# Attention units with four block pairs of keys: the fourth pair is transposed right behind the third

## The chip, the core and the metric

One core of a Trainium2 chip runs the whole kernel in one launch. The metric is device time in microseconds (us), and less is better. Engines in the text: TensorE (PE in the profile; its weight loads are PEld), VectorE (DVE), ScalarE (ACT), GpSimd (POOL) and SyncE (SP, which issues most DMAs). TensorE writes its results to PSUM, of which this kernel uses eight banks of 128 x 512 fp32; ScalarE and VectorE read them from there.

## The reference

One layer of a hybrid decoder, 1024 tokens by 1024 channels. One projection gives pool inputs, queries, keys, values and forget gates; half of the width goes through trailing means, the other half through causal attention with 8 heads of 64 channels and a bias from the gates. Then come an output projection with layer norm and an MLP with squared ReLU and a second layer norm.

```python
h = x @ w_in                                   # pool | q | k | v | forget gate
s = einsum('bhqd,bhkd->bhqk', q, k) * scale    # per head, causal
s = s + cq[..., :, None] - cf[..., None, :]    # cf = cumsum(log sigmoid(f))
p = softmax(where(kpos <= qpos, s, NEG_INF))
attn = einsum('bhqk,bhkd->bhqd', p, v)
x = layer_norm(ALPHA * x + concat([pool_out, attn]) @ w_out)
x = layer_norm(ALPHA * x + square(relu(x @ w_mlp1)) @ w_mlp2)
```

## The kernel before

All matrix products work on fp32 values that are split into a high and a low part (`split`: ScalarE copies the high part, VectorE subtracts to get the low part), and most take three matmuls (`three`).

Attention works by units `(p, e, m)`: head pair `p` (4), head `e` of it (2), and group `m` (4) of 256 queries. That is 32 units; for the first three head pairs a head's units run with m = 3, 2, 1, 0, for the last pair m rises. A unit with group m needs the keys of `m + 1` block pairs (a pair is 256 keys), so only a unit with m = 3 has four pairs; there are eight such units. For a unit, `att_probs` makes the scores on TensorE (L351, L352), adds the gate bias and takes the row minimum on VectorE (L357), and exponentiates on ScalarE (L359). One unit later `att_values` turns the probabilities and multiplies them with the values, all into one PSUM bank `ov` of the tag `pv`, of which there is one.

`turned(jp)` in `att_values` does one block pair: it takes a PSUM bank of tag `pt` (two buffers) and an SBUF tile `tt` of tag `A` (nine buffers), issues the transposes (L379: four, or three for a unit's last pair, the one on the diagonal), lets ScalarE copy the high part out (L380) and VectorE subtract the low part (L381). For the last pair GpSimd also clears a corner of `tt` (L377). The value passes of a pair are four matmuls of 256 columns (L395): two with the high part, which wait for L380, and two with the low part, which wait for L381. Once all passes are done, ScalarE and VectorE read `ov` (L400, L401) and SP stores the result (L402). Below, a unit's pairs are called first to fourth; "fourth turn" is the three transposes of the fourth pair, "third passes" are the four value passes of the third.

Between the passes, `fillstep` issues a piece of other TensorE work: the query and key projection of the next head pair (L83 to L85, bank tag `mm`), or in the last head pair the last pool group. After the units of the last head pair, the output projection follows.

The order on each engine is not that of the code: a scheduler fixes it before the run, engine by engine, from the code's order as a priority and from its own durations; it also puts in the semaphore waits and picks the buffers. Each engine then runs its list strictly in that order. In the code before, the second turn is issued ahead of the first passes, the third ahead of the second passes, and the fourth ahead of the third passes: one turn ahead at all times.

Of the kernel before, what the change touches and what calls it, by code (L numbers as in the profile page):

```python
# [36 lines left out]
def trunk(ctx, tc, xT, xn, wuqk, wvf, bf, poolw, pscale, wout, g1, b1, w1, w2, g2, b2, out):  # L37
# [13 lines left out]
    def slot(tag, shape, dt=F32R):  # L51
        uid[0] += 1
        return sb.tile([P] + list(shape), dt, tag=tag, bufs=NBUF[tag], name=f"{tag}{uid[0]}")
# [9 lines left out]
    def bank(tag=None):  # L63
        uid[0] += 1
        if tag is None:
            tag = CYCLE[rr[0] % 8]
            rr[0] += 1
        return ps.tile([P, CH], F32, tag=tag, bufs=PBUF[tag], name=f"{tag}{uid[0]}")
# [293 lines left out]
    def att_values(p, e, m, prob):  # L362
        h = 2 * p + e
        rows = slice(e * HD, (e + 1) * HD)
        orow = slice((1 - e) * HD, (2 - e) * HD)
        ov = bank("pv")[:, 0:256]

        def turned(jp):
            tp = bank("pt")
            tt = slot("A", [2, CH])  # L370
            if jp < m:
                blocks = [(jj * 256 + ii * P, 2 * jp + jj, ii) for jj in range(2) for ii in range(2)]
                ev = slice(0, CH)
            else:
                blocks = [(P, 2 * jp + 1, 1), (2 * P, 2 * jp, 0), (3 * P, 2 * jp, 1)]
                ev = slice(P, CH)
                nc.gpsimd.memset(tt[:, :, 0:P].bitcast(F32), 0.0)  # L377
            for col, j, ii in blocks:
                nc.tensor.transpose(tp[:, col : col + P], prob[ii][:, j * P : (j + 1) * P], ident)  # L379
            nc.scalar.copy(tt[:, 0, ev], tp[:, ev])  # L380
            nc.vector.tensor_tensor(tt[:, 1, ev], tp[:, ev], tt[:, 0, ev].bitcast(F32), ALU.subtract)  # L381
            return tt

        nxt = turned(0)
        for jp in range(m + 1):
            tt = nxt
            if jp < m:
                nxt = turned(jp + 1)
            fillstep()
            mov = ((0, 256), (256, CH)) if jp < m else ((256, CH), (0, 256))  # L390
            for s in range(2):
                for jj in range(2):
                    j = 2 * jp + jj
                    a, b = mov[jj]
                    nc.tensor.matmul(  # L395
                        ov, V[j][:, h].rearrange("p s d -> p (s d)"), tt[:, s, a:b],
                        start=(j == 0 and s == 0), stop=(j == 2 * m + 1 and s == 1),
                    )
        mx = slot("U", [256], F32)
        nc.scalar.copy(mx[rows], ov[orow])  # L400
        nc.vector.tensor_tensor(mx[rows], ov[rows], mx[rows], ALU.add)  # L401
        nc.sync.dma_start(mix_dram[m, rows, NG + p, :], mx[rows])  # L402
        if p == NPAIR - 1:
            row_scales(h, 2 * m, 2)
        elif m == 0:
            row_scales(h, 0, NT)

    def row_scales(h, i, n):
        ri = small([P, NT], "ri", bufs=2)
        nc.vector.reciprocal(ri[:, :n], rsum[h][:, i : i + n])  # L410
        tp = bank("pt")
        nc.tensor.transpose(tp[0:n, 0:P], ri[:, :n], ident)
        row = small([NT, P], "row")
        nc.scalar.copy(row[0:n], tp[0:n, 0:P])
        nc.sync.dma_start(rin_dram[h, i * P : (i + n) * P].rearrange("(i q) -> i q", q=P), row[0:n])
# [14 lines left out]
    def fillstep():  # L430
        fill["credit"] += fill["rate"]
        while fill["credit"] >= 1.0:
            fill["credit"] -= 1.0
            next(fill["gen"], None)
# [4 lines left out]
    for n, unit in enumerate(order):  # L439
        p = n // 8  # L440
        if n % 8 == 0:
            if p + 1 < NPAIR:
                gen, pieces, over = qk_proj(p + 1, "mm"), 4 * KT + 1, 28
            else:
                gen, pieces, over = last_fill(), (2 * KT + 2) * len(LATE), 14
            fill.update(gen=gen, credit=0.0, rate=pieces / over)
        prob = att_probs(*unit)
        if n + 1 < len(order):
            gate_row(2 * order[n + 1][0] + order[n + 1][1])
        if pend is None:  # L450
            for g in EARLY[1:]:
                pool_linear(g, "A")
        fillstep()
        if pend is not None:
            att_values(*pend)
        pend = (*unit, prob)
        if n % 8 == 7:
            run(gen)
    att_values(*pend)


# [390 lines left out]
    tt = nc.vector.tensor_tensor  # L852
# [303 lines left out]
```

## Time and profile before

| what | us |
|---|---|
| median of three runs (1041.37 to 1043.55) | 1042.59 |
| the profiled execution's own time | 1041.99 |
| its span, from the first instruction to the last | 1040.2 |
| TensorE busy in the span | 1018.5 |
| VectorE busy | 760.9 |
| ScalarE busy | 510.6 |

The attention units lie from about 117 to 326 us. The units with m = 3 have their passes at 120 (unit 1 below), 145 (2), 173 (3), 198 (4), 227 (5), 250 (6), 312 (7) and 319 us (8); 7 and 8 are those of the last head pair. In rows of the timeline, instructions of one line that follow each other on an engine are merged into one row: the first number is the start of the first, the second the time to the end of the last, `x4` their count, and brackets hold idle time of the engine before the row and what ended it. A matmul's shown duration is longer than its share of TensorE, since matmuls overlap; what one costs is read from the distance of the starts. On TensorE that is how a stall shows that leaves no idle time in the brackets.

### The profile page before, as it was taken

To read this page: it belongs to the slowest core of one execution; us is meant where nothing else is said; L and a number is where in the kernel's file an instruction comes from. 1 tells how busy PE (TensorE), PEld (TensorE's weight loads), DVE (VectorE), ACT (ScalarE), POOL (GpSimd) and SP (SyncE) were. 2 spreads that over 40 slices of the span, in tenths; PEclk is the share of its full clock that TensorE was granted. 3 is DMA by queue.
4 is the path that set the end of the run, shared out by engine and by line. 5 is a ranking of instruction groups with operands and counts; after the bars stand their busy time and mean duration, and the time that the engine had idled before them with its cause. 6 is when DMAs were issued, how large, how long until landed. Compare 5 with 4: busy or idle time off the path is not lost.

```text
span 1040.2 us, 14026 instructions
## 1 busy us (share of the span) xinstructions
PE 1018.5 (98%) x4976; PEld 846.2 (81%) x4976; DVE 760.9 (73%) x1303; ACT 510.6 (49%) x820; POOL 136.9 (13%) x236
## 2 busy tenths in 40 slices
PE   9999999999989999999999999999999999999996
PEld 9988888878768888887888888888788888888885
DVE  4576677777886897988888778788875566566547
ACT  4423666666774321676666766768631221122152
POOL 0000112111000021112122122120100000000047
PEclk9999999999999999999999999999999999999998
DMA  6302211111346542139757667565999888878753
GB/s 224 105 27 99 87 51 52 34 50 54 115 150 189 183 162 94 60 128 349 280 226 276 226 251 275 217 266 188 340 318 308 279 262 285 274 222 275 237 190 122
DMA packets 111798, 195.81 MB, mean 188 GB/s; under 512 B 9256, under 2 KB 77672, under 8 KB 111728
## 3 DMA queue, kind: packets, MB, share of 16 engines
q1 hardware_dynamic: 95456, 136.58, 40.2%
q0 software_dynamic: 15840, 57.68, 14.3%
q8 instruction: 39, 0.64, 0.3%
q10 hardware_dynamic: 432, 0.66, 0.2%
q14 instruction: 31, 0.25, 0.1%
HBM read 127.18 MB, written 67.70 MB: 187 GB/s over the span
## 4 chain that ended last, share of the span: by engine, by line
PE 52%; DVE 5%; DMA 2%; issue 1%; ACT 0%; DVEq 0%; SPq 0%
PE s L957 15%; PE s L603 9%; PE pv L957 8%; PE pt L603 6%; PE mm L603 6%; PE pv L603 4%; PE pt L957 2%; PE mm L957 2%; DMA S<-in_w_dram 1%; DVE B L72 1%; DMA A<-hid_dram 1%; DVE Q L72 0%; DVE A L726 0%; DVE bns L506 0%; DVE A L712 0%
## 5 line engine op out<-in xcount | busy, mean ns | idle before, releaser
L71 ACT CAST B<-S 128x1024 fp32r<-128x1024 f32 (+1 forms) x92 | 78.6, 871 | 171.4 <-DMA S<-in_w_dram 65.1
L603 PE MATMUL s<-B,Q 128*128 128x512 f32 x480 | 113.5, 389 | 0.1
L72 DVE TENSOR_TENSOR B<-S,B 128x1024 fp32r<-128x1024 f32 (+1 forms) x92 | 90.3, 994 | 28.2 <-ACT B L71 28.1
L603 PEld LDWEIGHTS s<-B,Q 128*128 128x128 f32 x480 | 90.0, 188 | 19.2 <-ACT B L71 0.6
L957 PE MATMUL s<-B,Q 128*128 128x512 f32 x390 | 94.8, 389 | 0.0
L957 PEld LDWEIGHTS s<-B,Q 128*128 128x128 f32 x390 | 73.2, 188 | 15.5
L71 ACT CAST Q<-S 128x1024 fp32r<-128x1024 f32 x52 | 54.6, 1051 | 62.8 <-PE s L603 17.0
L957 PE MATMUL s<-B,A 128*128 128x512 f32 x333 | 83.0, 394 | 1.2 <-DMA A<-hid_dram 1.2
L728 POOL DMA_DIRECT2D hid_dram<-A x90 | 48.4, 542 | 219.5 <-ACT A L725 175.5
L957 PEld LDWEIGHTS s<-B,A 128*128 128x128 f32 x333 | 62.4, 188 | 15.8 <-DMA A<-hid_dram 1.6
L72 DVE TENSOR_TENSOR Q<-S,Q 128x1024 fp32r<-128x1024 f32 x52 | 63.3, 1218 | 12.8 <-ACT Q L71 12.7
L603 PE MATMUL pt<-B,Q 128*128 128x512 f32 x300 | 71.6, 389 | 0.0
L603 PE MATMUL mm<-B,Q 128*128 128x512 f32 x300 | 71.6, 389 | 0.0
L395 PE MATMUL pv<-A,B 128*128 128x256 f32 x320 | 63.2, 299 | 4.8 <-ACT A L380 2.5
L395 PEld LDWEIGHTS pv<-A,B 128*128 128x128 f32 x320 | 50.2, 189 | 20.7 <-ACT A L380 9.7
L603 PEld LDWEIGHTS pt<-B,Q 128*128 128x128 f32 x300 | 56.3, 188 | 11.7
L603 PEld LDWEIGHTS mm<-B,Q 128*128 128x128 f32 x300 | 56.3, 188 | 11.7
L381 DVE TENSOR_TENSOR A<-pt,A 128x512 fp32r<-128x512 f32 (+1 forms) x80 | 49.0, 634 | 16.1 <-ACT A L380 15.5
L359 ACT ACTIVATE A<-A,nm 128x1024 f32<-128x1024 f32 (+7 forms) x64 | 49.7, 777 | 18.3 <-DVE nm L357 17.9
L726 DVE TENSOR_TENSOR A<-A,A 128x1024 f32<-128x1024 f32 x45 | 53.6, 1220 | 0.0
L344 POOL TENSOR_TENSOR A<-A,maskb 128x128 f32<-128x128 f32 x48 | 22.1, 460 | 232.3 <-DVE nm L357 135.8
L957 PE MATMUL pv<-B,Q 128*128 128x512 f32 x204 | 50.3, 390 | 0.0
(404 smaller groups left out, 2305.2 us busy)
## 6 DMA issues: line engine op xcount, KB each, us to landing
hid_dram<-A POOLq DMA_DIRECT2D x105, 512.0 KB, 3.9
S<-in_w_dram SPq DMA_DIRECT2D x62, 512.0 KB, 3.5
Q<-hid_dram SPq DMA_DIRECT2D x101, 256.0 KB, 4.5
A<-hid_dram SPq DMA_DIRECT2D x79, 256.0 KB, 4.8
S<-in_wuqk_dram SPq DMA_DIRECT2D x12, 512.0 KB, 3.2
A<-ncf_dram SPq DMA_DIRECT2D x8, 512.0 KB, 3.8
S<-in_wout_dram SPq DMA_DIRECT2D x8, 512.0 KB
S<-mix_dram SPq DMA_DIRECT2D x8, 512.0 KB, 5.3
```

The lines of the kernel that those rows point to most:

```text
L71: nc.scalar.copy(hi, src)
L72: nc.vector.tensor_tensor(lo, src, hi.bitcast(F32), ALU.subtract)
L344: nc.gpsimd.tensor_tensor(nb[:, qs], nb[:, qs], maskb, ALU.add)
L359: nc.scalar.activation(pt[:, :nk], pt[:, :nk], AF.Exp, bias=nm, scale=-1.0, accum_out=rsum[h][:, i : i + 1])
L381: nc.vector.tensor_tensor(tt[:, 1, ev], tp[:, ev], tt[:, 0, ev].bitcast(F32), ALU.subtract)
L395: nc.tensor.matmul(ov, V[j][:, h].rearrange("p s d -> p (s d)"), tt[:, s, a:b], start=(j == 0 and s == 0), stop=(j == 2 * m + 1 and s == 1),)
L603: nc.tensor.matmul(dst, b[x][:, k], A[a][y][:, k], start=first and k == 0 and i == 0, stop=k == H - 1 and i == 2, skip_group_check=not first,)
L726: nc.vector.tensor_tensor(x, x, hi.bitcast(F32), ALU.subtract)
L728: nc.gpsimd.dma_start(hid_dram[self.u, :, i, AT[name] : AT[name] + 2 * CH], part.rearrange("p q n t -> p (q n t)"))
L957: nc.tensor.matmul(dst, h[:, p_], w[q_], start=first and u == self.us[0] and j == 0, stop=u == self.us[-1] and j == 2, skip_group_check=no ...
```

## The change

In `att_values` the loop of turns is written anew. First and second turn are issued at the start (as before, where the second came ahead of the first `fillstep`); at the second pair, all turns that are left are issued, ahead of the `fillstep` and the passes of the second pair. With m = 2 that is one turn, the third, where it was before. Only with m = 3 does anything move: the fourth turn is issued behind the third turn instead of behind the second passes.

```diff
-        nxt = turned(0)
+        tts = {}
         for jp in range(m + 1):
-            tt = nxt
-            if jp < m:
-                nxt = turned(jp + 1)
+            if jp == 0:
+                tts[0] = turned(0)
+                if m:
+                    tts[1] = turned(1)
+            elif jp == 1:
+                for nxt in range(2, m + 1):
+                    tts[nxt] = turned(nxt)
+            tt = tts[jp]
             fillstep()
```

Line numbers behind this place rise by 6 (L395 becomes L401, L400 becomes L406). What the scheduler makes of it, by engine: on TensorE the lists differ in the eight units with m = 3 and, behind unit 5, in the unit after it; on ScalarE and VectorE the lists differ in unit 5 and the unit after it alone; on GpSimd and SP the order is the same.

In units 2, 3, 7 and 8 the fourth turn moves past all four second passes. TensorE in unit 2, before; `pt_1527` and `pt_1542` are the banks of the third and fourth turn, `pv_1500` is `ov`, `A_1510` the second pair's tile, `A_1528` the third's:

```order
L379 MATMUL pt_1527<-ident_63,A_1419 128x128
L379 MATMUL pt_1527<-ident_63,A_1406 128x128
L395 MATMUL pv_1500<-A_1510,B_401 128x256 x4
L379 MATMUL pt_1542<-ident_63,A_1406 128x128
L379 MATMUL pt_1542<-ident_63,A_1419 128x128
L379 MATMUL pt_1542<-ident_63,A_1406 128x128
L83 MATMUL mm_1452<-B_429,B_1449 128x512
```

The same place after (the fourth turn's bank is now `pt_1535`):

```order
L379 MATMUL pt_1527<-ident_63,A_1419 128x128
L379 MATMUL pt_1527<-ident_63,A_1406 128x128
L379 MATMUL pt_1535<-ident_63,A_1406 128x128
L379 MATMUL pt_1535<-ident_63,A_1419 128x128
L379 MATMUL pt_1535<-ident_63,A_1406 128x128
L401 MATMUL pv_1500<-A_1510,B_401 128x256 x4
L83 MATMUL mm_1452<-B_429,B_1449 128x512
```

Seven transposes stand in a row, the second passes follow them, and what comes next is as before.

In units 1, 4, 5 and 6 the fourth turn moves past the last two of the second passes only. TensorE in unit 4, before; `A_2124`, `A_2139` and `A_2154` are the tiles of the second, third and fourth pair:

```order
L395 MATMUL pv_2114<-A_2124,B_401 128x256 x2
L84 MATMUL mm_2051<-B_436,B_2048 128x512
L85 MATMUL mm_2051<-B_436,B_2048 128x512
L395 MATMUL pv_2114<-A_2124,B_401 128x256 x2
L379 MATMUL pt_2153<-ident_63,A_2017 128x128
L379 MATMUL pt_2153<-ident_63,A_2030 128x128
L379 MATMUL pt_2153<-ident_63,A_2017 128x128
L395 MATMUL pv_2114<-A_2139,B_467 128x256 x2
```

And after, where the fourth pair has `pt_2146`:

```order
L401 MATMUL pv_2114<-A_2124,B_401 128x256 x2
L84 MATMUL mm_2051<-B_436,B_2048 128x512
L85 MATMUL mm_2051<-B_436,B_2048 128x512
L379 MATMUL pt_2146<-ident_63,A_2017 128x128
L379 MATMUL pt_2146<-ident_63,A_2030 128x128
L379 MATMUL pt_2146<-ident_63,A_2017 128x128
L401 MATMUL pv_2114<-A_2124,B_401 128x256 x2
L401 MATMUL pv_2114<-A_2139,B_467 128x256 x2
```

The last two second passes and the fourth turn have changed places; the third passes start behind both, as before.

In unit 5 ScalarE's list changes too. Before; `A_2447`, `A_2462` are the tiles of the third and fourth pair, `A_2491` and `A_2499` probabilities of a later unit, `A_2516` the first pair's tile of the unit that follows, `pv_2422` this unit's `ov`:

```order
L380 CAST A_2447<-pt_2446 128x512
L305 CAST Q_2354<-mm_2362 64x512
L359 ACTIVATE A_2491,rsum_2277<-A_2491,nm_2495 128x512
L380 CAST A_2462<-pt_2461 128x384
L359 ACTIVATE A_2499,rsum_2277<-A_2499,nm_2503 128x384
L380 CAST A_2516<-pt_2515 128x512
L400 COPY U_2486<-pv_2422 64x256
```

After, with `A_2455` as the fourth pair's tile:

```order
L380 CAST A_2447<-pt_2446 128x512
L305 CAST Q_2354<-mm_2362 64x512
L380 CAST A_2455<-pt_2454 128x384
L359 ACTIVATE A_2491,rsum_2277<-A_2491,nm_2495 128x512
L406 COPY U_2486<-pv_2422 64x256
L359 ACTIVATE A_2499,rsum_2277<-A_2499,nm_2503 128x384
L380 CAST A_2516<-pt_2515 128x512
```

The fourth pair's copy goes ahead of one exponential, and the copy of `ov` and a second exponential now stand ahead of the next unit's first copy (`A_2516`). On TensorE the four fourth passes, which stood in two parts around the first four transposes and three projection matmuls of the next unit, stand together and ahead of all of these; the next unit's first eight transposes follow them in a row, then three projection matmuls (L84, L85, L83), then its first passes. On VectorE the subtraction of the fourth pair goes ahead of the score step of `A_2499`.

## Rows read from the trace of the kernel before

**Rows 1.** The page's first part: busy us, share of the span and instructions of each engine.

```profile
PE 1018.5 (98%) x4976; PEld 846.2 (81%) x4976; DVE 760.9 (73%) x1303; ACT 510.6 (49%) x820; POOL 136.9 (13%) x236
```

**Rows 2.** The list of waits of TensorE from 110 to 330 us: instruction and line, what it waited for, us in total, times, longest.

```profile
PE pv L395 <- ACT A L380: 2.5, 5, 1.3
PE pv L395 <- DVE A L381: 1.8, 4, 0.7
```

**Rows 3.** The timeline of TensorE in unit 1: third turn, two second passes, two projection matmuls, two second passes, fourth turn, third passes, a projection matmul, fourth passes.

```profile
121.11 0.60 PE L379 MATMUL pt<-ident,A 128*128 128x128 f32 x4
...
122.25 0.40 PE L395 MATMUL pv<-A,B 128*128 128x256 f32 x2
122.48 0.49 PE L379 MATMUL pt<-ident,A 128*128 128x128 f32 x3
122.73 0.94 PE L395 MATMUL pv<-A,B 128*128 128x256 f32 x4
123.50 0.40 PE L83 MATMUL mm<-B,B 128*128 128x512 f32 x1
...
124.18 0.64 PE L395 MATMUL pv<-A,B 128*128 128x256 f32 x4
```

**Rows 4.** The timeline of VectorE in unit 1: the low parts of the second and the third pair.

```profile
121.32 0.69 DVE L381 TENSOR_TENSOR A<-pt,A 128x512 fp32r<-128x512 f32 x1 [0.60 <-ACT A L380]
122.41 0.69 DVE L381 TENSOR_TENSOR A<-pt,A 128x512 fp32r<-128x512 f32 x1 [0.40 <-ACT A L380]
```

**Rows 5.** The timeline of TensorE in unit 2, the four second passes, straight behind the third turn.

```profile
147.06 0.73 PE L395 MATMUL pv<-A,B 128*128 128x256 f32 x4
```

**Rows 6.** The timeline of TensorE in unit 3: the first two third passes.

```profile
176.18 0.51 PE L395 MATMUL pv<-A,B 128*128 128x256 f32 x2 [0.16 <-ACT A L380]
```

**Rows 7.** The timeline of TensorE in unit 4, a projection matmul and the fourth passes, and its next long wait, in the unit behind; then the same wait behind unit 6.

```profile
201.29 0.39 PE L85 MATMUL mm<-B,B 128*128 128x512 f32 x1
201.53 0.73 PE L395 MATMUL pv<-A,B 128*128 128x256 f32 x4
...
208.38 0.39 PE L395 MATMUL pv<-A,B 128*128 128x256 f32 x1 [0.69 <-DVE A L381]
...
261.05 0.51 PE L395 MATMUL pv<-A,B 128*128 128x256 f32 x2 [0.70 <-DVE A L381]
```

**Rows 8.** The timeline of ScalarE and VectorE behind that projection matmul, and the busy time of each engine from there to the end of the wait at 208.38 (columns: stretch, us, busy time of PE, PEld, DVE, ACT, POOL with counts, granted TensorE clock, DMA share, GB/s).

```profile
201.72 0.59 ACT L316 ACTIVATE Q<-mm 64x512 fp32r<-64x512 f32 x1 [0.61 <-PE mm L85]
202.35 0.68 DVE L317 SCALAR_TENSOR_TENSOR Q<-mm,Q 64x512 fp32r<-64x512 f32 x1 [0.65 <-ACT Q L316]
...
202.30:208.30 6.00, 5.39 (x29) 4.17 (x27) 5.75 (x13) 3.47 (x9) 1.35 (x3) 1.00 0.04 11
```

**Rows 9.** The timeline of TensorE in unit 5, from the next unit's first transposes to the end of the part whose order changes.

```profile
230.42 0.38 PE L379 MATMUL pt<-ident,A 128*128 128x128 f32 x2
231.01 0.50 PE L395 MATMUL pv<-A,B 128*128 128x256 f32 x2 [0.22 <-ACT A L380]
231.35 0.38 PE L379 MATMUL pt<-ident,A 128*128 128x128 f32 x2
...
236.33 0.40 PE L83 MATMUL mm<-B,B 128*128 128x512 f32 x1
```

**Rows 10.** The timeline of ScalarE in unit 5.

```profile
229.03 0.58 ACT L305 CAST Q<-mm 64x512 fp32r<-64x512 f32 x1
229.64 0.72 ACT L359 ACTIVATE A<-A,nm 128x512 f32<-128x512 f32 x1
230.48 0.48 ACT L380 CAST A<-pt 128x384 fp32r<-128x384 f32 x1
230.86 0.62 ACT L359 ACTIVATE A<-A,nm 128x384 f32<-128x384 f32 x1
...
231.77 0.59 ACT L380 CAST A<-pt 128x512 fp32r<-128x512 f32 x1 [0.21 <-PE pt L379]
232.71 0.37 ACT L400 COPY U<-pv 64x256 f32<-64x256 f32 x1 [0.35 <-PE pv L395]
```

**Rows 11.** The timeline of VectorE in unit 5: the low parts of the third and fourth pair.

```profile
229.04 0.69 DVE L381 TENSOR_TENSOR A<-pt,A 128x512 fp32r<-128x512 f32 x1
...
230.99 0.56 DVE L381 TENSOR_TENSOR A<-pt,A 128x384 fp32r<-128x384 f32 x1
```

**Rows 12.** The timeline of VectorE (low parts of the first two pairs) and of TensorE (third turn) in unit 8.

```profile
320.46 1.28 DVE L381 TENSOR_TENSOR A<-pt,A 128x512 fp32r<-128x512 f32 x2
321.54 0.60 PE L379 MATMUL pt<-ident,A 128*128 128x128 f32 x4
```

**Rows 13.** Busy time of each engine in stretches (columns as in rows 8): the attention units up to the lower clock, eight transposes in a row in unit 1, the stretch at a lower clock, and the stretch of unit 7 with eight transposes and a long wait behind them.

```profile
117.00:302.50 185.50, 180.02 (x1059) 148.15 (x1058) 143.21 (x350) 122.76 (x269) 29.36 (x76) 1.00 0.21 68
118.50:119.30 0.80, 0.80 (x10) 0.80 (x9) 0.63 (x3) 0.80 (x1) 0.59 (x2) 1.00 1.00 348
302.50:305.90 3.40, 3.39 (x9) 2.81 (x10) 3.40 (x8) 1.97 (x3) 0.00 (x0) 0.50 0.43 143
309.70:313.20 3.50, 1.98 (x15) 1.53 (x14) 2.99 (x8) 3.41 (x7) 0.31 (x1) 1.00 0.64 206
```

**Rows 14.** The timeline of TensorE just ahead of the stretch at the lower clock.

```profile
300.32 0.73 PE L83 MATMUL mm<-Q,U 128*128 128x512 f32 x2 [1.24 <-ACT Q L71]
...
302.51 0.79 PE L84 MATMUL mm<-Q,U 128*128 128x512 f32 x1 [0.92 <-DVE Q L72]
```

## The prediction

> **What bounds the kernel now.** The page's busy line comes first: TensorE is busy for 1018.5 of 1040.2 us, VectorE for 73% and ScalarE for 49% [rows 1]. So a change of order wins only what TensorE idles or stalls for, and loses whatever new stall it makes. The list of TensorE's waits says how much that can be in attention: the value passes wait 2.5 us in all for ScalarE's copies and 1.8 us for VectorE's subtractions [rows 2], over all 32 units. Only eight units change, so I went through these eight on TensorE's timeline and looked, in each, which turn the waiting passes wait for. Last I read the granted clock: 1.00 in attention up to 302.5 us, then 0.50 for one stretch [rows 13].
>
> **The swap, units 1 to 4 and 6 to 8.** No instruction is added or removed; 24 transposes (eight units, three each) change places with two or four value passes. Prices: a transpose costs 0.11 us (the four in unit 1 take 0.60, of which 0.27 is the last one's own length, leaving 0.33 for three steps), a value pass 0.12 (four take 0.64, 0.28 of it the last one's), a projection matmul 0.23 (three between 123.50 and 124.18) [rows 3]. The third passes stand behind both the second passes and the fourth turn before and after. They start at the same time, and the third turn, whose results they need, has not moved. A stall in front of the third passes therefore stays. In unit 1 the four take 0.94 from 122.73, against 0.73 in the same position behind transposes in unit 2 [rows 3, 5]: they lose 0.2 because VectorE has the third pair's low part only at 122.41 + 0.69 = 123.10 [rows 4]. In unit 3 they idle 0.16 for ScalarE's copy of the third pair [rows 6]. Neither is touched: zero.
>
> What does come sooner is the fourth pair, by two passes (0.24 us) or four (0.47). Only the fourth passes use it. In unit 1 they run without a stall already (0.64 at 124.18 [rows 3]); units 2, 3, 7 and 8 have no stall there either. In unit 4 they take 0.73 instead of 0.64 [rows 7], so 0.1 us goes away, and the same in unit 6. What is late next: TensorE idles 0.69 us at 208.38, and 0.70 at 261.05, for a subtraction of VectorE [rows 7]. VectorE's work up to there starts from the projection matmul at 201.29 (copied at 201.72, taken up by VectorE at 202.35) and keeps VectorE busy for 5.75 of 6.00 us [rows 8]. That matmul stands ahead of the fourth passes, so VectorE doesn't start sooner, and the 0.1 us turns into a longer idle time at 208.38. Both units: zero.
>
> **The new wait.** A turn's bank is one of two. The fourth turn takes the second turn's, so it must wait until VectorE has subtracted the second pair; before, the passes ahead of it had waited for the same. In unit 1 that is done at 121.32 + 0.69 = 122.01 [rows 4], and the fourth turn's new place is 122.25, where the last two second passes stood [rows 3]: 0.24 us to spare. In unit 8 it is done at 320.46 + 1.28 = 321.74, and the new place is 321.54 + 4 x 0.11 = 321.98 [rows 12]: again 0.24. The same two views give the other six as much or more. Zero here, with small cover.
>
> **Unit 5.** Here the scheduler's lists differ on three engines. In the trace TensorE loses 0.48 us on the fourth passes: from 230.42 to 231.35 are 0.93 us, in which two transposes (0.22) and two passes (0.23) ran [rows 9]. They wait for ScalarE's copy, which at 230.48 stands behind the exponential of 229.64 [rows 10]. Now the copy follows the one that ends at 229.03 + 0.58 = 229.61, and runs to 230.12 (0.48 long). VectorE is free at 229.04 + 0.69 = 229.73 [rows 11], so it subtracts from 230.15 to 230.71 (0.56). The first two fourth passes start at 230.42 without a wait; the third would start at 230.65 and waits to about 230.77, and a pass behind a wait costs 0.1 more (the two at 231.01 take 0.34 to the next start, not 0.23 [rows 9]). Lost: 0.22. Gain: 0.48 - 0.22 = 0.26.
>
> The price stands behind it. The fourth passes end together at about 231.11; the next unit's eight transposes (0.88) and three projection matmuls (0.69) follow, and its first pass is due at 232.68. It needs ScalarE's copy of its first pair. ScalarE has before that copy, in its new list: the exponential (230.14 to 230.98; from start to next start the row of 229.64 took 0.84), the copy of `ov`, which waits for the last fourth pass and so runs from 231.30 to 231.67 (0.37), the shorter exponential (0.62 and some 0.1 for its sum, to 232.4), and only then the copy of 0.59 [rows 10], to about 232.95. TensorE's pass starts at about 233.0 and pays 0.1 more: 0.4 lost. The third turn of that unit then has little between itself and its passes: 0 to 0.15. Sum: -0.26 + 0.4 + (0 to 0.15) = +0.1 to +0.3; I take +0.2, since the wait for the copy is worked out from ScalarE's own rows and nothing else covers it. It stands at -0.26 if ScalarE gets through its list in time, at +0.5 if the first pass of the unit behind waits for the subtraction also. The part ended at 236.33 [rows 9], and from there on the lists are equal. TensorE runs from there up to 253 us without a long wait, and the next one, at 261.05, begins from a projection matmul on TensorE's own pace, like that at 208.38 [rows 7, 8]. So the 0.2 us is carried on.
>
> GpSimd's and SP's lists don't change. Buffers of tag `A` come in another turn, by which some copies behind the eight units wait for ScalarE's instruction before them; no row prices that, but an exponential that starts 0.1 before the copy ahead of it ends (230.48 + 0.48 against 230.86 [rows 10]) shows what such an overlap is worth: 0 to 0.1 in six units. No pass waits for these copies in most of them; I take 0, and 0.6 as the upper bound.
>
> **Sum.** The profiled execution took 1041.99 us, 1.8 more than its span and 0.6 less than the median of the runs, 1042.59. Seven units give 0, unit 5 gives +0.2: 1042.2 on that execution's scale, 1042.8 on the median's. That is no change: a measurement of this kernel can tell about 0.2%, or 2.1 us, from none.
>
> **The rivals.**
> *All waits of the eight units go, and the gain is carried to the end.* 0.2 (unit 1), 0.3 (unit 3, its idle 0.16 and what follows a wait), 0.1 (4), 0.5 (5) and 0.1 (6) are 1.2 us: 1041.4. Against it: the third passes wait for the third turn, which stays. [...]
>
> *The new wait decides.* The fourth turn waits for VectorE in front of passes that used to run, and everything on TensorE queues behind it: second passes, third passes, the projection. The price of such a wait is some 0.3 us (idle 0.22 plus 0.1, as in unit 5 [rows 9]), eight times 2.4: 1045.0, slower. It decides when VectorE frees the bank 0.24 us later than now, or when TensorE's queue needs that long from the end of a subtraction to a transpose. For it speaks that the cover is equal and thin in units 1 and 8; against it, that passes in unit 5 started 0.05 us after the copy they waited for (230.48 + 0.48, start at 231.01).
>
> [...]
>
> [...]
>
> **How the numbers follow.** The forecast, 1042.8, has a chance of 0.76; all waits gone 0.08; the new wait 0.06; the clock 0.10. The range goes from 1041.0 (the all-waits rival, and the runs' own spread of 1.2 below the median) to 1044.5 (one more fall of the clock). Faster by over 0.2% (under 1040.5) is half of the first rival: 0.04. Slower by over 0.2% (over 1044.7) is two thirds of the new wait and less than half of the clock: 0.08. The rest, 0.88, is no measurable change.
>
> **What would show it.** Right: the third passes of units 1 and 3 stall as before; the fourth passes of units 4 and 6 take 0.64, and the idle times at 208.4 and 261 grow by 0.1; in unit 5 the fourth passes run with a short stall and the next unit's first pass idles some 0.3 for ScalarE; the projection matmul at 236.33 comes 0.1 to 0.3 later; attention has one stretch at a clock of 0.50. Wrong: an idle time ahead of a fourth turn, which is the new wait; a second stretch at 0.50, or none; or a shift that arises behind 326 us, where no list differs.

## The result and the profile after

| | median us | ratio to the kernel before, 95% interval |
|---|---|---|
| kernel before (17 runs) | 1041.75 | |
| changed kernel (17 runs, 1041.82 to 1045.79) | 1043.40 | 1.0016 (1.0010 to 1.0023) |

The change costs 1.65 us, 0.16%: less than the 0.2% that was called no change, and yet its interval doesn't reach 1. The profiled execution is the slowest of the 17, 1045.79 us with a span of 1044.0, so its total is not compared; its parts are. In the experiments one execution of `fifth_alone` (2619.97 us) and one of the kernel before (3606.91 us) are slow ones; all ratios, and the median of `fifth_alone`, leave them out.

The page's busy line and TensorE's waits from 110 to 330 us, kernel after, and below them the same waits of `null_change`, an experiment of the next section that has the instructions of the kernel before:

```profile
PE 1020.1 (98%) x4976; PEld 845.9 (81%) x4976; DVE 760.7 (73%) x1303; ACT 509.0 (49%) x820; POOL 137.0 (13%) x236
```

```profile
PE pv L401 <- ACT A L380: 3.2, 4, 1.4
PE pv L401 <- DVE A L381: 1.7, 4, 0.7
```

```profile
PE pv L403 <- ACT A L380: 3.4, 5, 1.4
PE pv L403 <- DVE A L381: 1.6, 3, 0.7
```

The value passes wait 4.9 us in all, against 4.3 before [rows 2]: the waits that the new order could have taken away are still there. The 0.6 us more can't be put down to the change, since `null_change` has 5.0. TensorE's timeline in units 1, 3 and 4, and the next long waits behind units 4 and 6:

```profile
121.58 0.49 PE L379 MATMUL pt<-ident,A 128*128 128x128 f32 x3
121.82 1.16 PE L401 MATMUL pv<-A,B 128*128 128x256 f32 x6
122.83 0.39 PE L83 MATMUL mm<-B,B 128*128 128x512 f32 x1
...
175.42 0.50 PE L401 MATMUL pv<-A,B 128*128 128x256 f32 x2 [0.16 <-ACT A L380]
...
200.49 0.39 PE L85 MATMUL mm<-B,B 128*128 128x512 f32 x1
200.72 0.63 PE L401 MATMUL pv<-A,B 128*128 128x256 f32 x4
...
207.57 0.51 PE L401 MATMUL pv<-A,B 128*128 128x256 f32 x2 [0.68 <-DVE A L381]
...
260.33 0.50 PE L401 MATMUL pv<-A,B 128*128 128x256 f32 x2 [0.55 <-DVE A L381]
```

In unit 1 the last two second and the four third passes take 1.01 us to the next matmul; before, with the fourth turn between them, they took 0.23 and 0.77 [rows 3]. The loss only moved by some passes. In unit 3 the idle 0.16 is still there [rows 6]. No row has idle time ahead of a fourth turn. In unit 4 the fourth passes now take 0.63, and the wait behind ends 7.08 us after the projection matmul (200.49 to 207.57); before it was 7.09 (201.29 to 208.38 [rows 7]). The 0.1 us was given back.

Unit 5, TensorE and then ScalarE:

```profile
229.20 0.40 PE L83 MATMUL mm<-B,B 128*128 128x512 f32 x1
229.43 1.08 PE L401 MATMUL pv<-A,B 128*128 128x256 f32 x6
230.35 1.04 PE L379 MATMUL pt<-ident,A 128*128 128x128 f32 x8
...
231.69 0.40 PE L83 MATMUL mm<-B,B 128*128 128x512 f32 x1
232.19 0.51 PE L401 MATMUL pv<-A,B 128*128 128x256 f32 x2
232.54 0.39 PE L84 MATMUL mm<-B,B 128*128 128x512 f32 x1
...
234.50 0.40 PE L85 MATMUL mm<-B,B 128*128 128x512 f32 x1
234.81 0.51 PE L401 MATMUL pv<-A,B 128*128 128x256 f32 x2
235.16 0.28 PE L351 MATMUL s<-Q,Q 128*128 128x256 f32 x1
...
235.87 0.40 PE L83 MATMUL mm<-B,B 128*128 128x512 f32 x1
...
240.51 0.39 PE L351 MATMUL s<-Q,Q 128*128 128x512 f32 x1
```

```profile
228.88 0.48 ACT L380 CAST A<-pt 128x384 fp32r<-128x384 f32 x1
229.25 0.73 ACT L359 ACTIVATE A<-A,nm 128x512 f32<-128x512 f32 x1
...
230.55 0.37 ACT L406 COPY U<-pv 64x256 f32<-64x256 f32 x1 [0.48 <-PE pv L401]
230.82 0.61 ACT L359 ACTIVATE A<-A,nm 128x384 f32<-128x384 f32 x1
...
231.55 1.07 ACT L380 CAST A<-pt 128x512 fp32r<-128x512 f32 x2
```

Two third and four fourth passes take 0.92 us where six times 0.115 are 0.69: 0.23 lost. The next unit's first pass, due 0.23 after 231.69, starts at 232.19, once the first of ScalarE's two copies from 231.55 is done: 0.27 late, and 0.35 instead of 0.23 for its two passes. The first two of the four last passes of that next unit (234.81) are 0.08 late and lose 0.12 more. What the unit costs is read from the lead over the kernel before, where the first and the last of these matmuls stand at

```profile
229.96 0.39 PE L83 MATMUL mm<-B,B 128*128 128x512 f32 x1
...
241.06 0.39 PE L351 MATMUL s<-Q,Q 128*128 128x512 f32 x1
```

Ahead of the part whose order changes, the lead is 0.76 us (229.96 against 229.20; nearly all of it arises in the first 10 us, ahead of any change). The matmul that stood at 236.33 [rows 9] is at 235.87: a lead of 0.46. At 240.51 it is 0.55. So unit 5 costs 0.30 where its part ends, and 0.21 of it is carried on.

Two more things differ, both behind unit 6. First the clock (columns as in rows 8), kernel after:

```profile
302.00:306.00 4.00, 3.18 (x18) 2.48 (x17) 3.92 (x10) 3.36 (x7) 0.00 (x0) 1.00 0.58 220
753.37:756.78 3.41, 3.41 (x10) 2.65 (x9) 2.29 (x3) 0.00 (x0) 0.00 (x0) 0.50 1.09 362
```

The stretch at 0.50 is gone from attention [rows 13] and stands at 753 us. Second, the last stage, the second matrix product of the MLP. In the timeline of TensorE the same two rows, 1,026 matmuls apart, in the kernel before:

```profile
787.46 2.43 PE L957 MATMUL mm<-B,Q 128*128 128x512 f32 x10
...
1022.22 1.53 PE L957 MATMUL s<-B,A 128*128 128x512 f32 x6
```

and in the kernel after:

```profile
790.39 2.46 PE L963 MATMUL mm<-B,Q 128*128 128x512 f32 x10
...
1026.02 1.55 PE L963 MATMUL s<-B,A 128*128 128x512 f32 x6
```

234.76 us before, 235.63 after: 0.87 us more for the same matmuls at a clock of 1.00, without an idle time in either.

### The profile page after: what moved, and what is told of

The parts are those of the page before. It is cut to its first block, busy times and chain, and to the rows that moved or that the text cites. A ratio compares the mean times of both kernels' runs of the same rounds, so it can differ in the third digit from the quotient of the medians.

```text
span 1044.0 us, 14027 instructions
## 1 busy us (share of the span) xinstructions
PE 1020.1 (98%) x4976; PEld 845.9 (81%) x4976; DVE 760.7 (73%) x1303; ACT 509.0 (49%) x820; POOL 137.0 (13%) x236
## 4 chain that ended last, share of the span: by engine, by line
PE 52%; DVE 4%; DMA 2%; issue 1%; ACT 0%; DVEq 0%; SPq 0%; ACTq 0%
PE s L963 15%; PE s L609 9%; PE pv L963 8%; PE pt L609 6%; PE mm L609 6%; PE pv L609 4%; PE pt L963 2%; PE mm L963 2%; DMA S<-in_w_dram 1%; DVE B L72 1%; DMA A<-hid_dram 1%; DVE A L732 0%; DVE Q L72 0%; ACT Q L71 0%; DVE bns L512 0%
## 5 line engine op out<-in xcount | busy, mean ns | idle before, releaser
L401 PE MATMUL pv<-A,B 128*128 128x256 f32 x320 | 62.7, 298 | 5.4 <-ACT A L380 3.2
L401 PEld LDWEIGHTS pv<-A,B 128*128 128x128 f32 x320 | 49.2, 188 | 21.4 <-ACT A L380 11.0
```

Of the source, the lines that this page charges most:

```text
L401: nc.tensor.matmul(ov, V[j][:, h].rearrange("p s d -> p (s d)"), tt[:, s, a:b], start=(j == 0 and s == 0), stop=(j == 2 * m + 1 and s == 1),)
```

## The experiments

**First question: which unit costs, and is it real?** Theory A is the prediction's: unit 5 costs 0.3 us, the rest is scatter. Theory B: the change acts by way of the buffers of ring `A` (the nine buffers of tag `A`, handed out as they come free), and the cost shows as a stall at 354 us, which stands in the profile after:

```profile
354.24 0.66 PE L582 MATMUL s<-ident,A 128*128 128x128 f32 x4 [1.62 <-DVE A L537]
```

Four kernels. `same_again` is the changed kernel. The other three put a condition into it, and leave the fourth turn where it was for the other units; in `fifth_alone`:

```diff
             elif jp == 1:
-                for nxt in range(2, m + 1):
+                for nxt in range(2, (m + 1) if (p == 2 and e == 0) else min(m + 1, 3)):
                     tts[nxt] = turned(nxt)
+            elif jp == 2 and m == 3 and not ((p == 2 and e == 0)):
+                tts[3] = turned(3)
```

`all_but_fifth` has the condition negated, `null_change` has `False`.

`same_again`. 

> The changed kernel once more, for a second profile. Theory A (the cost is the queue of ScalarE in the fifth of the eight units, 0.3 us, and the rest of the first difference of 1.65 us is scatter): the difference comes out smaller than before, 0.3 to 1.0 us (ratio 1.0003 to 1.0010), and the stall at 354 us (TensorE 1.62 us idle for VectorE, which waits for a load of x) isn't there in this profile, or is there in profiles of either kernel. Theory B (the stall at 354 us belongs to the change, by way of other buffers for the turned blocks): 1.65 us again (1.0010 to 1.0023), with the stall at 354 us in this profile too.

Measured: 1043.20 against 1041.69 us, 1.0014 (1.0005 to 1.0024).

`null_change`. 

> The changed code with its condition set so that no unit is changed: the same instructions as the kernel before, with other line numbers. Both theories: 0 us, ratio 1.0000 within 0.0006. If it is slower by 0.5 us or more, the comparison itself has an error of that size and a difference of 1.65 us can't be put down to the change. A stall of over 1 us at 354 us in this profile speaks for theory A.

Measured: 1041.88, 1.0004 (0.9993 to 1.0014).

`fifth_alone`. 

> The change in the fifth unit alone (head 4, the queries of m=3); the other seven stand as before. Theory A: +0.3 us (1.0003), the projection matmul in the next unit 0.3 us later against the matmuls ahead of the unit, and nothing more up to the end. Theory B: +0.3 us in the unit, and the stall at 354 us only if the load of x (A_3791, A_3879) or the load of the gates is the cause by a wait that the fifth unit adds: here the gates' load alone has the added wait for GpSimd, so 0.3 us with the stall absent. If the whole 1.65 us come from the fifth unit by a later collision: 1.0012 to 1.0020.

Measured: 1041.77, 1.0004 (0.9995 to 1.0013).

`all_but_fifth`. 

> The change in all units but the fifth. Theory A: 0 us (0.9997 to 1.0003), the fourth units' 0.1 us of gain given back at the next copy, no loss in any unit. Theory B: +1.3 us (1.0010 to 1.0016), with the stall at 354 us, since the load of x here has the added wait for GpSimd as in the whole change.

Measured: 1043.14, 1.0016 (1.0008 to 1.0025).

The cost is real, and theory A falls: the kernel in which only the seven units that were put at zero are changed is 1.45 us slower, and the fifth alone, at 0.08, can't be told from none. Theory B falls in its second half. `all_but_fifth` has no stall at 354 us; the largest one between 340 and 400 us is 0.43, in `same_again` 0.94 at 379, in `null_change` and `fifth_alone` none.

What all these profiles share is the last stage. The two rows shown above, in `null_change`, `fifth_alone` and `all_but_fifth`, one fence each:

```profile
786.35 2.43 PE L965 MATMUL mm<-B,Q 128*128 128x512 f32 x10
...
1021.11 1.53 PE L965 MATMUL s<-B,A 128*128 128x512 f32 x6
```

```profile
787.55 2.43 PE L965 MATMUL mm<-B,Q 128*128 128x512 f32 x10
...
1021.70 1.54 PE L965 MATMUL s<-B,A 128*128 128x512 f32 x6
```

```profile
788.49 2.46 PE L965 MATMUL mm<-B,Q 128*128 128x512 f32 x10
...
1024.22 1.56 PE L965 MATMUL s<-B,A 128*128 128x512 f32 x6
```

234.76, 234.15 and 235.73 us. `null_change` has the kernel before's figure to the hundredth and `same_again` (235.62) that of the changed kernel. This is no scatter: each program has its own pace there. The lists of instructions are equal in this stage; what differs on TensorE is the addresses of tiles of ring `A`. The buffers lie 4,160 bytes apart. A tile takes the free one when it is first written, so one tile that is made earlier in unit 1 gives most of the later ones another buffer. In the last stage four of the nine hold sums of the output, and the other five take turns with blocks of the MLP's hidden layer, which are weights of the matmuls of L957 (other blocks lie in ring `Q`). By the addresses in the built programs these five are 0, 1, 3, 7, 8 in the kernel before, 0, 2, 3, 4, 7 after, 0, 1, 4, 7, 8 in `fifth_alone` and 0, 2, 4, 6, 7 in `all_but_fifth`.

**Second question: is it where these blocks lie (theory S), or the order in the units (theory O)?** Here the ring is moved without touching a unit: spare tiles of ring `A` are written with one column by GpSimd, so that the buffers are handed out from another point. First ahead of the output projection (in `before_moved` one tile, in `before_better` four, `before_memsets` seven, and in `after_moved` six, on the changed kernel):

```diff
+    for _ in range(1):
+        dummy = slot("A", [D], F32)
+        nc.gpsimd.memset(dummy[:, 0:1], 0.0)
     gam, bet = load_row("Q", g1), load_row("Q", b1)
```

`before_moved`. 

> The kernel before with one memset of one column into a spare buffer of the ring A on GpSimd, ahead of the output projection: no unit of attention is changed, but the ring is handed out one buffer further, and the hidden blocks of the last stage lie in buffers 0, 2, 3, 4 and 7, as in the changed kernel, and no longer in 0, 1, 3, 7 and 8. Theory S (the cost of the change is where these blocks lie: TensorE's weight loads from some of the nine buffers are slower): 0.7 to 1.4 us slower than before (1.0007 to 1.0014), nearly all of it spread over 715 to 1030 us, matmuls with a block of ring A as weights 232 ns apart on the mean and not 230. Theory O (the cost is the order of transposes and value passes in the seven units): 0 us (1.0000 within 0.0005).

Measured: 1042.74 against 1041.91, 1.0009 (1.0000 to 1.0019).

`after_moved`. 

> The changed kernel with six such memsets: the units stay as changed, the hidden blocks of the last stage lie in buffers 1, 4, 6, 7 and 8. By the distances of matmuls on each buffer in the profiles so far (227.8 ns on 1, 230 on 0, 4 and 8, 233 on 2, 3, 6 and 7) this set costs as much as that of the kernel before. Theory S: +0.3 to +0.6 us against the kernel before (1.0003 to 1.0006), of which 0.3 us are the fifth unit. Theory O: +1.5 us (1.0010 to 1.0020).

Measured: 1044.57, 1.0022 (1.0013 to 1.0031).

`before_better`. 

> The kernel before with four such memsets: hidden blocks of the last stage in buffers 0, 1, 3, 4 and 8. Theory S: 0.3 to 0.6 us faster than before (0.9994 to 0.9997), from 715 us on. Theory O, or a cost of the memsets: 0 us or slower.

Measured: 1042.76, 1.0005 (0.9993 to 1.0016).

`before_memsets`. 

> The control: the kernel before with seven such memsets, after which the ring stands as in the kernel before, and the hidden blocks lie in buffers 0, 1, 3, 7 and 8 as there. Theory S and theory O: 0 us (1.0000 within 0.0005), the matmuls from 715 us on at the distances of the kernel before. If it is slower by over 0.5 us, the memsets and their waits have a price of their own, which the other three then also carry.

Measured: 1044.77, 1.0031 (1.0020 to 1.0042).

The control failed: seven memsets cost 2.9 us by themselves. Against `null_change`, instruction by instruction, the kernels with six and seven lose 3.1 and 2.2 us between 326 and 400 us, ahead of the stage in question. So the totals of the other three, of which `after_moved` and `before_better` lie above what theory S gave them, say nothing, and only the pace of the last stage can be read. There the control is exact:

```profile
789.67 2.43 PE L960 MATMUL mm<-B,Q 128*128 128x512 f32 x10
...
1024.43 1.54 PE L960 MATMUL s<-B,A 128*128 128x512 f32 x6
```

234.76 us again, with the blocks in the kernel before's buffers. `before_moved` (235.58), `before_better` (234.20) and `after_moved` (234.83) have the paces that theory S gives to their buffers.

**The same, with the memsets at places where they cost little**, inside attention: one in unit 4 of the changed kernel (`n == 12`, `after_cheap`), on the kernel before two in the first (`n == 24`, `before_dear`), one in the second (25, `before_cheap`) and one in the third unit of the last head pair (26, `before_spare`, the control):

```diff
         prob = att_probs(*unit)
+        if n == 12:
+            for _ in range(1):
+                spare = slot("A", [S], F32)
+                nc.gpsimd.memset(spare[:, 0:1], 0.0)
```

`after_cheap`. 

> The changed kernel with one memset of one column on GpSimd into a spare buffer of ring A, in the fourth of the eight units. No engine's order changes but by this memset. The hidden blocks of the last stage come to lie in buffers 0, 3, 4, 5 and 8; buffer 5 held none so far and is put, as a guess from the buffers next to it in address, at the 228 ns of buffer 1. Theory S (the buffers in which the last stage's weights lie cost the time): from 715 us on 0.5 to 0.8 us less than the kernel before, some 1.9 us less than the changed kernel; in all 0.3 us for the fifth unit against it, so 0.0 to 0.5 us faster than the kernel before (0.9995 to 1.0000) and 1.5 us faster than the changed kernel. Theory O (the order in the seven units): 1.5 us slower than the kernel before (1.0010 to 1.0020).

Measured: 1041.98 against 1041.99, 0.9999 (0.9990 to 1.0008).

`before_dear`. 

> The kernel before with two such memsets, in the first unit of the last pair of heads: hidden blocks of the last stage in buffers 1, 2, 3, 6 and 7, of which four are the slow ones. Theory S: 0.9 to 1.2 us slower than before (1.0008 to 1.0012), spread over 715 to 1030 us. Theory O: 0 us.

Measured: 1043.64, 1.0014 (1.0004 to 1.0024).

`before_cheap`. 

> The kernel before with one such memset, in the second unit of the last pair: hidden blocks in buffers 0, 1, 3, 5 and 8. Theory S: 0.8 to 1.4 us faster than before (0.9987 to 0.9993) from 715 us on; faster than both kernels. Theory O, or no effect of where the blocks lie: 0 us.

Measured: 1041.58, 0.9992 (0.9984 to 1.0001).

`before_spare`. 

> The control for the memset: the kernel before with one such memset in the third unit of the last pair, after which the hidden blocks lie in buffers 0, 1, 3, 7 and 8, as in the kernel before. Both theories: 0 us (1.0000 within 0.0005), and distances from 715 us on as in the kernel before. If it is slower by more, the memset has a price of its own in attention, which the other three then also carry.

Measured: 1041.80, 0.9999 (0.9988 to 1.0010).

The two rows in `after_cheap`, `before_dear` and `before_cheap`:

```profile
788.18 2.43 PE L967 MATMUL mm<-B,Q 128*128 128x512 f32 x10
...
1022.27 1.52 PE L967 MATMUL s<-B,A 128*128 128x512 f32 x6
```

```profile
786.47 2.46 PE L961 MATMUL mm<-B,Q 128*128 128x512 f32 x10
...
1022.12 1.56 PE L961 MATMUL s<-B,A 128*128 128x512 f32 x6
```

```profile
786.24 2.43 PE L961 MATMUL mm<-B,Q 128*128 128x512 f32 x10
...
1020.06 1.52 PE L961 MATMUL s<-B,A 128*128 128x512 f32 x6
```

All of it in one table (stretch: distance of the two rows; difference: of the medians on the same chip, while the ratios above are estimates of their own and differ from the ratios of the medians by up to 0.0004):

| kernel | units | buffers of the blocks | stretch us | difference us |
|---|---|---|---|---|
| `before_cheap` | before | 0 1 3 5 8 | 233.82 | -0.41 |
| `after_cheap` | after | 0 3 4 5 8 | 234.09 | -0.01 |
| `fifth_alone` | fifth changed | 0 1 4 7 8 | 234.15 | +0.08 |
| `before_spare` | before | 0 1 3 7 8 | 234.61 | -0.19 |
| kernel before, `null_change` | before | 0 1 3 7 8 | 234.76 | 0, +0.19 |
| after, `same_again` | after | 0 2 3 4 7 | 235.63, 235.62 | +1.65, +1.51 |
| `before_dear` | before | 1 2 3 6 7 | 235.65 | +1.65 |
| `all_but_fifth` | seven changed | 0 2 4 6 7 | 235.73 | +1.45 |

The kernel before with the blocks in bad buffers is as slow as the changed one, and the changed kernel with the blocks in good buffers is as fast as the kernel before. Theory O is out: it gave `after_cheap` 1.0010 at least, and its interval ends at 1.0008. `before_dear` and `before_cheap`, whose units are those of the kernel before, are 2.06 us apart, and their stretches 1.83. Theory S holds in sign in the four totals that are clear of noise, all of them slower, and in size within the intervals (with unit 5 where it is changed), though `before_dear` and `all_but_fifth` lie 0.8 and 0.5 us above what the stretch alone gives. Counted from 713 us, where this product starts, their profiles lose 1.15 and 1.49 us against `null_change`, with the waits for loads that the stretch leaves out. `before_cheap` is the best version found; that it beats the kernel before is not shown, since its interval reaches 1.0001.

## Why the prediction was right, and where it was not

- *Class and range*: no measurable change, and 1043.40 lies in 1041.0 to 1044.5, 0.6 above the forecast. That it lies so near is in part luck: the forecast started from a median of three runs, 1042.59, which 17 runs put at 1041.75. The change itself was put at +0.2 us and measured at +1.65.
- *The swap in units 1 to 4 and 6 to 8*: as predicted on TensorE. The stalls of units 1 and 3 stayed, the 0.1 of unit 4 was given back within 7 us, though at the passes of 205.00, where the lead falls from 0.91 to 0.81; the idle time at the end shows 0.68, not the 0.8 that was named. In unit 6 the profile after shows an idle time of 0.55 instead of 0.70, but that isn't the change: it is 0.68 in `same_again` and 0.71 in `all_but_fifth`, and 0.52 in `before_spare`, whose units are those of the kernel before.
- *The new wait*: none, as predicted; the 0.24 us of cover held.
- *Unit 5*: right, with each term near its measure: fourth passes 0.23 lost (0.22 predicted), the next unit's first passes 0.27 late and 0.12 longer (0.4), its last ones 0.2 (0 to 0.15), in sum 0.30 where its part ends and 0.21 from 240 us on, where 0.1 to 0.3 was given and 0.2 taken. `fifth_alone` shows it in the trace, not in its total, since its blocks lie in buffers that are 0.6 us cheaper.
- *The step that failed*, though the class and the range came out right, is the paragraph on buffers: "Buffers of tag `A` come in another turn ... I take 0, and 0.6 as the upper bound". It looked for the price in waits, in the copies next to the change. The price is 0.87 us, in a stage 450 us later, without any wait: the matmuls there start further apart on the mean, those whose weights came to lie in another buffer by up to 3.5 ns. No row read for the prediction showed that matmuls of one form have more than one pace there.
- *The shift behind 326 us* was named as a sign of a wrong prediction, and that is what came. Unit 5 (0.21) and the last stage (0.87) are 1.1 of the 1.65 us (1.0 to 2.4 by the interval). The rest is open: both profiles of the changed kernel also lose 1.4 to 1.5 us against `null_change` between 326 and 400 us, at other places in each (354 and 379 us), while `all_but_fifth` loses 0.1 there and `after_cheap`, with all eight units changed, 0.3. So the new order alone doesn't bring it; whether the changed kernel's buffers do, or it is scatter, wasn't tried.
- *The clock*: wrong both ways in the profile. The stretch at 0.50 in attention vanished and one came at 753 us. But it can't be put down to the change: `null_change`, the same instructions as the kernel before, has none in attention either. Seven transposes in a row in unit 7, just behind a stretch in which TensorE was busy for 1.99 of 3.50 us (308.3 to 311.8), ran at 1.00. The range's upper end of 1044.5, the chance of 0.10 and part of the 0.08 hold one more fall by way of the new order, put at 1.7 us at most (half of the 3.4 us at 0.50 [rows 13]), and the 0.04 for faster holds one fall less by it. No run shows either term: in its place the profile after shows 1.00 from 117 to 326 us, and `null_change`, without the new order, 1.00 from 302 to 306 us.

## What to carry to other kernels

A change of order can also change which buffer later tiles get, so a difference of a tenth of a per cent can arise in a stage that the change doesn't touch (here 0.87 us in the last one); compare the distance of the same two instructions in every stage before a reason is sought at the place of the edit. A control that should be empty can have a price of its own (here 2.9 us), and then only the part of the trace that it can't reach may be read.

## What the hardware showed

**The pace of matmuls goes by the buffer of their weights.** Mean distance from a matmul of 512 columns to the next, by the buffer of ring `A` that holds its weights, 787 to 1024 us, all 14 profiles of these programs, 192 to 1,115 matmuls each:

| buffer | 0 | 1 | 2 | 3 | 4 | 5 | 6 | 7 | 8 |
|---|---|---|---|---|---|---|---|---|---|
| ns | 229.7 | 227.6 | 233.2 | 233.0 | 229.9 | 227.2 | 233.2 | 232.8 | 229.7 |

Three levels, and every fourth buffer has the same: 1 and 5; 0, 4 and 8; 2 and 6, 3 and 7. Four buffers are 16,640 bytes. Buffer 5 was put at 228 before it was measured. The rows show a pace that goes by the weights' buffer, 227.2 to 233.2 ns; what brings it about was not tried.

The address of a matmul's own weights isn't all of it. Of the 1,026 matmuls between the two rows, 468 have their weights in ring `A` and 558 in ring `Q`, the latter at the same addresses in every kernel. Of the 0.87 us, 0.57 lie at the first and 0.30 at the second. What else in ring `A` takes part (the sums, the loads of the next blocks) these runs don't tell apart.

**The clock's fall moves between executions of the same instructions.** In the kernel before the clock is 0.50 from 302.5 us on [rows 13], behind TensorE's idle times of 1.24 and 0.92 us [rows 14]; `null_change` has 1.24 and 0.93 there and stays at 1.00. Between 751.8 and 753.4 us the clock fell to 0.50 in the profiles of the changed kernel, `same_again` and `before_better`, where TensorE had waited 1.56, 2.32 and 2.35 us for loads of hidden blocks right there, and in none of the others, where it had waited 1.07 to 1.34.
